# Low parts of weights all on VectorE from the output projection on, and the first feed-forward weights split earlier

## Chip, cores and metric

The kernel runs on one core of a Trainium2 chip. The metric is device time in microseconds (us), the median of several executions; lower is better. Engines: TensorE (PE) multiplies, VectorE (DVE) and ScalarE (ACT) work on vectors, GpSimd (POOL) does too but can't read PSUM, SyncE (SP) only starts DMAs. Each engine takes its instructions in order.

## What is computed

One layer of a hybrid block on x (512 x 1024, float32): token mixing with three branches, cross-attention into 256 memory tokens, a SwiGLU feed-forward, each inside two RMS norms with a residual. Cut to its core:

```python
h = rms_norm(x, g_mix_pre)
lru_x, lru_gate, pool_in, q, k, v, q_idx, k_idx, w_idx, gate_logits = split_columns(h @ w_in, IN_SIZES)
up = einsum(stack([ya, yb, yc]), w_branch)            # ya, yb, yc: the three mixers
merged = sum(sigmoid(gate_logits + b_gate) * up)
x = x + rms_norm(merged @ w_out, g_mix_post)
h = rms_norm(x, g_mem_pre); m = rms_norm(mem, g_mem_kv)
q = h @ w_mem_q; k, v = split(m @ w_mem_kv, 2)        # 4 heads of 128
o = softmax(q @ k.T * 128 ** -0.5) @ v
x = x + rms_norm(o @ w_mem_o, g_mem_post)
h = rms_norm(x, g_ffn_pre)
f_gate, f_up = split(h @ w_ffn_in, 2)                 # 2816 columns each
x = x + rms_norm((silu(f_gate) * f_up) @ w_ffn_out, g_ffn_post)
```

## The kernel before

**Products in three parts.** Each float32 operand is cut into a rounded high part and a low part, the rest. `mm3` (L89 to L92) issues three matmuls for a product: high by high, high by low, low by high. So every weight needs a split ahead of its matmuls. `split_next` (L182) does it: ScalarE casts `raw` to the high part `wh` (L191), then the low part `wl` = raw - wh is made either by one VectorE subtraction over 1024 columns (L195) or by two GpSimd subtractions over 512 each (L198, L199). Which of the two is a list: `low_on("v")` sends all that follow to VectorE, `"g"` all to GpSimd, `"vg"` one after the other.

**Weights in a row.** The weights are a fixed list of 128x1024 pieces: ..., eight of w_out, four K and four V pieces of w_mem_kv, four of w_mem_q, four of w_mem_o, then the feed-forward's. In the names they are numbered: w_out 59 to 66, K 67 to 70, V 71 to 74, w_mem_q 75 to 78, w_mem_o 79 to 82, feed-forward 83 on. Six `raw` buffers are loaded by SyncE as they come free, that is after the low part is made; there are four buffers for high and four for low parts. `take_w` hands out the next weight and splits two ahead; `prefetch(n)` splits up to n ahead. The first four feed-forward weights (`NFIRST`) go into free larger buffers (`K8`), so these can be split before the four pairs are free.

**The stretch around the change.** TensorE's work in program order: the output projection (`project`, hold 2: the last two weights are done row block by row block, t = 0 to 3); K (m = 0 to 3) and V (i = 0 to 3) of the memory; the four heads of w_mem_q with scores, softmax and the products with V (`mem_scores`, `mem_tr`, `mem_av`); w_mem_o (hold 4); the first four feed-forward weights in two column halves (rows 0 to 255 of the tokens, then 256 to 511).
Between them runs a chain per row block, class `Residual`, called R[t]: sums of squares on ScalarE (L286) and the gain on VectorE (L907), the inverse root `rstd` (VectorE L271, L273, L275; GpSimd's power step L274; VectorE L278, L279), the residual (L923), squares again, `rstd` again, the normalised rows (L932), then `turn`: transposes on TensorE (L294), high part `hh` on ScalarE (L302) and low part `hl` on VectorE (L303). The next product reads `hh` and `hl`. `halves` (L392, L393) cuts a PSUM result the same way on ScalarE and VectorE.

**What sets the order.** The program is written in one sequence; a list scheduler puts it into a fixed order per engine at build time, by priority (roughly the place in the program, with splits raised or lowered by `high_priority`) and by its own estimate of times. So a changed engine for one step can move others past each other.

Of the kernel before, what the change touches and what calls it, by code (L numbers as in the profile page):

```python
# [18 lines left out]
KD = D // P  # L19
# [11 lines left out]
NFIRST = 4  # L31
# [34 lines left out]
def hybrid_block_kernel(ctx: ExitStack, tc: tile.TileContext, a: dict, out: bass.AP):  # L66
# [22 lines left out]
    def mm3(o, lh, ll, rh, rl, start, stop):  # L89
        T.matmul(o, lh, rh, start=start, stop=False, skip_group_check=True)  # L90
        T.matmul(o, lh, rl, start=False, stop=False, skip_group_check=True)  # L91
        T.matmul(o, ll, rh, start=False, stop=stop, skip_group_check=True)  # L92
# [6 lines left out]
    def pump(ns):  # L99
        while bg and ns > 0:  # L100
            cost, fn = bg.popleft()
            fn()
            ns -= cost

    def drain_bg():
        while bg:
            bg.popleft()[1]()
# [71 lines left out]
    def low_on(engines):  # L179
        low[:] = engines  # L180

    def split_next(pin=False):  # L182
        src = raws.popleft()
        shape = list(specs[state["split"]][0])
        if first_ffn <= state["split"] < first_ffn + NFIRST:
            both = K8.take([P, 2] + shape[1:], F32R)
            h, l, back = both[:, 0], both[:, 1], lambda: K8.give(both)
        else:
            th, tl = WH.take(shape, F32R), WL.take(shape, F32R)
            h, l, back = th, tl, lambda: (WH.give(th), WL.give(tl))  # L190
        copy = A.copy(h, src)  # L191
        if pin:
            tc.keep_in_program_order(copy)
        if low[state["low"] % len(low)] == "v":
            V.tensor_sub(l, src, f32(h))  # L195
        else:
            c = shape[1] // 2
            G.tensor_sub(l[:, :c], src[:, :c], f32(h[:, :c]))  # L198
            G.tensor_sub(l[:, c:], src[:, c:], f32(h[:, c:]))  # L199
        state["low"] += 1  # L200
        RAW.give(src)
        state["split"] += 1
        ready.append((h, l, back))
        load_ahead()

    def prefetch(ahead=None, pin=False):
        want = state["taken"] + (LOOKAHEAD if ahead is None else ahead)
        while (state["split"] < min(len(specs), want) and raws
               and (WH.free or first_ffn <= state["split"] < first_ffn + NFIRST)):
            with tc.high_priority(offset=-100):  # L210
                split_next(pin)

    def take_w(ahead=None):
        while state["split"] <= state["taken"]:
            split_next()
        w = ready.popleft()
        state["taken"] += 1
        prefetch(ahead)
        return w

    def give_w(*ws):
        for w in ws:
            w[2]()
# [159 lines left out]
    def unit_piece(o, w, c0, c1, ks=range(KD)):  # L383
        for k in ks:
            mm3(o[:, c0:c1], w[0][:, k], w[1][:, k], hh[:, k, c0:c1], hl[:, k, c0:c1], k == 0, k == KD - 1)

    def unit(o, w):
        unit_piece(o, w, 0, S)
        give_w(w)

    def halves(src, h, l):
        A.copy(h, src)  # L392
        V.tensor_sub(l, src, f32(h))  # L393
# [91 lines left out]
    for m in range(1, 4):  # L485
        w = take_w()
        ps = PS.take([P, S])
# [14 lines left out]
    w = take_w()  # L502
    ps = PS.take([P, S])
# [25 lines left out]
    for i, name in enumerate(("lru_w_a", "lru_w_x")):  # L529
        t = T2.take([P, 4, P])  # L530
# [6 lines left out]
    t = T2.take([P, 4, P])  # L537
# [108 lines left out]
    for m in range(4):  # L646
        w = take_w()
        ps = PS.take([P, S])
# [5 lines left out]
    for g in GROUPS:  # L654
        w = take_w()
        ps = PS.take([P, S])
# [9 lines left out]
    for m in range(4):  # L666
        w = take_w()
        ps = PS.take([P, S])
# [140 lines left out]
    for m in range(4):  # L809
        w = take_w()  # L810
        ps = PS.take([P, S])
# [46 lines left out]
        bg.append((1, f))  # L858
    low_on("vg")
    branch(2, yc, lambda: pump(1))  # L860
    low_on("g")
    drain_bg()
    K8.give(*yc, *acc, mem)
    GB.give(g_kv)
# [98 lines left out]
    for m in range(4):  # L963
        w = take_w()
        ps = PS.take([P, NM])
# [19 lines left out]
    for i in range(4):  # L985
        w = take_w()
        for kk in range(2):
            k = 2 * i + kk
# [6 lines left out]
        if i == 2:  # L995
            R[2].turn()
    R[3].turn()
    low_on("v")
    for t in range(2):
        halves(pv[t], vmem[:, 0, t], vmem[:, 1, t])  # L1000
    PS.give(*pv)
# [9 lines left out]
    def mem_scores(h):  # L1011
        mx, sm = col(4, "mx4"), col(4, "sm4")
        pss = []
        for i in range(2):
            ps = PS.take([P, 2, NM])
            pss.append(ps)
            for j in range(2):
                r = slice((2 * i + j) * P, (2 * i + j + 1) * P)
                mm3(ps[:, j], qm[0][:, h, r], qm[1][:, h, r], kmem[:, 0, h], kmem[:, 1, h], True, True)
            V.tensor_reduce(mx[:, 2 * i:2 * i + 2], ps, axis=AX.X, op=OP.max)  # L1020
        V.tensor_scalar(mx, mx, -mscale, None, op0=OP.mult)
        pt = [T2.take([P, 2, NM]) for _ in range(2)]
        for t in range(4):
            A.activation(pt[t // 2][:, t % 2], pss[t // 2][:, t % 2], AF.Exp, bias=mx[:, t:t + 1], scale=mscale,
                         accum_out=sm[:, t:t + 1])
        V.reciprocal(sm, sm)
        for t in range(4):
            p_ = pt[t // 2][:, t % 2]
            V.tensor_scalar(p_, p_, sm[:, t:t + 1], None, op0=OP.mult)
        PS.give(*pss)  # L1030
        mprob[h] = pt

    def mem_tr(h):
        pt = mprob.pop(h)
        hl_ = K8.take([P, 2, 2, S], F32R)
        for kb in range(2):
            ps = PS.take([P, S])
            for t in range(4):
                T.transpose(ps[:, t * P:(t + 1) * P], pt[t // 2][:, t % 2, kb * P:(kb + 1) * P], ident)
            halves(ps, hl_[:, 0, kb], hl_[:, 1, kb])  # L1040
            PS.give(ps)
        T2.give(*pt)
        mprob[h] = hl_
# [11 lines left out]
    for h in range(4):  # L1055
        w = take_w()
        ps = PS.take([P, S])
        for k in range(KD):
            mm3(ps, w[0][:, k], w[1][:, k], hh[:, k], hl[:, k], k == 0, k == KD - 1)
            if k == 5 and h >= 1:  # L1060
                mem_scores(h - 1)
            if k == 5 and h >= 2:
                mem_tr(h - 2)
        give_w(w)
        halves(ps, qm[0][:, h], qm[1][:, h])
        PS.give(ps)
    low_on("vg")
    mem_av(0)
    mem_av(1)
    mem_scores(3)  # L1070
    K8.give(*qm, kmem)
    mem_tr(2)

    HH.give(hh)
    HL.give(hl)
# [2 lines left out]

    def after_o(t, pss):
        R.append(Residual(t, pss, g_post, g_next))  # L1080
        if t == 0:
            low_on("g")
            prefetch(4 + NFIRST)
        if t == 2:
            R[0].scale2()
            R[0].norm()
        if t >= 1:
            R[t - 1].add()
            R[t - 1].square()
        R[t].scale()  # L1090
# [51 lines left out]
        if c == 0:  # L1142
            R[3].turn()
    give_w(*ws)
    low_on("g")
    for m in range(NFIRST // 2):
        swiglu(m, pss[2 * m], pss[2 * m + 1])
    GB.give(g_post, g_next)
    g_post = gain("g_ffn_post")
    for m in range(NFIRST // 2, NFF):  # L1150
        if m == NFIRST // 2 + 1:
            low_on("v")
        w0, w1 = take_w(), take_w()
        pg, pu = PS.take([P, S]), PS.take([P, S])
        unit(pg, w0)
        unit(pu, w1)
        swiglu(m, pg, pu)
# [52 lines left out]
```

## Time and profile before

| | us |
|---|---|
| median of 3 runs | 917.13 (917.04 to 917.58) |
| profiled execution | 914.67 |
| its span, first to last instruction | 912.9 |
| TensorE busy (4179 matmuls) | 885.9, 97% of the span |
| VectorE busy | 499.8, 55% |
| ScalarE busy | 344.3, 38% |
| GpSimd busy | 231.2, 25% |
| subtractions of low parts: VectorE L195, 79 of them | 98.2 |
| GpSimd L198 and L199, 65 pairs | 88.9 and 91.8 |

Busy times are sums over an engine; matmuls overlap a little, and their ends are modelled. Stretches of the trace: the output projection ends at 437.7 us, K and V run to about 467, the heads to about 510, w_mem_o to 537.7, then the feed-forward. A timeline row gives start, duration, engine, line, operation and tiles, and in brackets the engine's idle time before it with what ended it. Buffer numbers are left out of tile names there.

### The profile page before, as it was taken

What the parts mean: (1) busy time and instruction counts of PE and PEld (TensorE: products, weight loads), DVE (VectorE), ACT (ScalarE), POOL (GpSimd) and SP (SyncE); (2) the same over time, 40 slices, a digit from 0 to 9 for tenths busy, and PEclk for the clock granted to TensorE, in tenths of its full rate; (3) what the DMA queues carried; (4) which work ended last, traced back from release to release, by engine and by line L of the source; (5) the groups of instructions that cost most, each with busy time, mean ns of one, the idle gap of its engine ahead of it and who ended that gap; (6) DMA issues with size and microseconds to landing.
All of it is one profiled execution on the core that took longest, in us unless ns stands there. A gap on an engine that the chain in (4) does not pass through costs nothing.

```text
span 912.9 us, 11068 instructions
## 1 busy us (share of the span) xinstructions
PE 885.9 (97%) x4179; PEld 730.5 (80%) x4179; DVE 499.8 (55%) x889; ACT 344.3 (38%) x575; POOL 231.2 (25%) x203
## 2 busy tenths in 40 slices
PE   7999999999999999999989989999999999999997
PEld 6788888888788788888868779888888888888885
DVE  5769989946773745311876783433334443222225
ACT  4465553225654544322655452222223222211121
POOL 2223464644444322344561460000000000000000
PEclk9999999999999999999999999999999999999999
DMA  8953237333332245333454230333333332333102
GB/s 245 242 128 93 70 93 184 93 94 91 104 81 77 75 150 185 96 107 97 117 161 115 70 116 1 93 93 98 104 97 93 93 93 92 96 99 104 48 1 93
DMA packets 122801, 95.42 MB, mean 105 GB/s; under 512 B 5568, under 2 KB 111612, under 8 KB 122748
## 3 DMA queue, kind: packets, MB, share of 16 engines
q1 hardware_dynamic: 120172, 90.52, 34.5%
q10 hardware_dynamic: 2576, 4.19, 1.3%
q8 instruction: 33, 0.54, 0.2%
q14 instruction: 20, 0.16, 0.1%
HBM read 86.83 MB, written 2.10 MB: 97 GB/s over the span
## 4 chain that ended last, share of the span: by engine, by line
PE 88%; DVE 5%; issue 2%; ACT 2%; POOL 1%; DMA 1%; ACTq 0%; DVEq 0%; SPq 0%; POOLq 0%
PE ps L91 28%; PE ps L90 28%; PE ps L92 28%; PE ps L450 1%; PE ps L775 1%; PE ps L760 1%; PE ps L294 1%; DVE wl L195 1%; DVE hl L303 1%; DVE k L932 1%; POOL wl L199 1%; POOL y L274 1%; DVE c L278 0%; DVE k L393 0%; DMA k<-t 0%
## 5 line engine op out<-in xcount | busy, mean ns | idle before, releaser
L191 ACT CAST wh<-raw 128x1024 fp32r<-128x1024 f32 (+1 forms) x144 | 150.5, 1047 | 388.9 <-issue 154.3
L91 PE MATMUL ps<-hl,wh 128*128 128x512 f32 (+2 forms) x736 | 285.5, 388 | 3.7 <-DVE hl L303 3.7
L90 PE MATMUL ps<-hh,wh 128*128 128x512 f32 (+2 forms) x736 | 285.9, 389 | 0.3 <-ACT hh L302 0.3
L92 PE MATMUL ps<-hh,wl 128*128 128x512 f32 (+2 forms) x736 | 285.4, 388 | 0.0
L195 DVE TENSOR_TENSOR wl<-raw,wh 128x1024 fp32r<-128x1024 f32 x79 | 98.2, 1243 | 163.0 <-ACT wh L191 163.0
L91 PEld LDWEIGHTS ps<-hl,wh 128*128 128x128 f32 (+1 forms) x736 | 137.6, 187 | 34.0 <-DVE hl L303 4.6
L90 PEld LDWEIGHTS ps<-hh,wh 128*128 128x128 f32 (+1 forms) x736 | 137.4, 187 | 30.0 <-ACT hh L302 0.5
L92 PEld LDWEIGHTS ps<-hh,wl 128*128 128x128 f32 (+1 forms) x736 | 137.5, 187 | 29.7
L198 POOL TENSOR_TENSOR wl<-raw,wh 128x512 fp32r<-128x512 f32 (+1 forms) x65 | 88.9, 1368 | 199.4 <-ACT wh L191 178.2
L274 POOL TENSOR_TENSOR y<-u,half 128x1 f32<-128x1 f32 x26 | 15.1, 587 | 415.5 <-DVE u L271 384.6
L199 POOL TENSOR_TENSOR wl<-raw,wh 128x512 fp32r<-128x512 f32 (+1 forms) x65 | 91.8, 1412 | 0.0
L90 PE MATMUL ps<-wh,k 128*128 128x512 f32 x192 | 75.8, 395 | 0.0
L91 PE MATMUL ps<-wl,k 128*128 128x512 f32 x192 | 75.5, 393 | 0.0
L92 PE MATMUL ps<-wh,k 128*128 128x512 f32 x176 | 69.7, 396 | 0.0
L90 PE MATMUL ps<-k,wh 128*128 128x512 f32 (+1 forms) x128 | 47.2, 369 | 0.0
L1128 DVE TENSOR_TENSOR t<-t,ps 128x512 f32<-128x512 f32 x22 | 15.1, 688 | 58.5 <-PE ps L92 58.5
L92 PE MATMUL ps<-k,wl 128*128 128x512 f32 (+1 forms) x128 | 46.9, 366 | 0.0
L92 PE MATMUL ps<-wh,x 128*128 128x512 f32 x112 | 44.2, 395 | 0.0
L91 PEld LDWEIGHTS ps<-wl,k 128*128 128x128 f32 x192 | 36.1, 188 | 8.1
L90 PEld LDWEIGHTS ps<-wh,k 128*128 128x128 f32 x192 | 36.0, 188 | 8.2
L92 PEld LDWEIGHTS ps<-wh,k 128*128 128x128 f32 x176 | 33.4, 190 | 8.1 <-DVE k L393 0.2
L90 PE MATMUL ps<-wh,x 128*128 128x512 f32 x96 | 38.8, 404 | 0.0
(210 smaller groups left out, 1173.7 us busy)
## 6 DMA issues: line engine op xcount, KB each, us to landing
raw<-in_w_in SPq DMA_DIRECT2D x45, 512.0 KB, 4.0
raw<-in_w_ffn_in SPq DMA_DIRECT2D x44, 512.0 KB, 3.8
raw<-in_w_ffn_out SPq DMA_DIRECT2D x22, 512.0 KB, 3.5
raw<-in_w_branch SPq DMA_DIRECT2D x12, 512.0 KB, 3.4
k<-t SPq DMA_DIRECT2D x32, 128.0 KB, 2.4
raw<-in_w_out SPq DMA_DIRECT2D x8, 512.0 KB, 3.6
raw<-in_w_mem_kv SPq DMA_DIRECT2D x8, 512.0 KB, 3.6
k<-in_x ACTq DMA_DIRECT2D x2, 1024.0 KB, 8.9
```

What stands on the lines that cost most here:

```text
L90: T.matmul(o, lh, rh, start=start, stop=False, skip_group_check=True)
L91: T.matmul(o, lh, rl, start=False, stop=False, skip_group_check=True)
L92: T.matmul(o, ll, rh, start=False, stop=stop, skip_group_check=True)
L191: copy = A.copy(h, src)
L195: V.tensor_sub(l, src, f32(h))
L198: G.tensor_sub(l[:, :c], src[:, :c], f32(h[:, :c]))
L199: G.tensor_sub(l[:, c:], src[:, c:], f32(h[:, c:]))
L274: G.tensor_tensor(y, u, half, op=OP.pow)
L294: T.transpose(ps[:, k], src[:, (4 * q + k) * P:(4 * q + k + 1) * P], ident)
L303: V.tensor_sub(hl[:, 4 * q:4 * q + 4, dst], ps, f32(h))
L450: T.matmul(ps[:, :n], q[j][:, hp, r], k[i][:, :n], start=i == 0, stop=i == 1, skip_group_check=True)
L1128: V.tensor_mul(th, th, pu)
```

## The change

`low_on("v")` now stands right behind the third branch, where `low_on("g")` stood, and the later switches are gone: every low part from weight 61 on is made by VectorE (the first ones of these while the third branch still runs). 24 weights move: 61 to 76, 82, 84 to 86 and 87 to 90. The first head of w_mem_q is multiplied in two column halves of 256 tokens, 48 matmuls instead of 24. `prefetch(4 + NFIRST)` is called ahead of w_mem_o instead of behind its first row block. (With h = 0 the scores call of the loop isn't reached, so `h >= 1` is no longer written.)

```diff
--- before.py
+++ after.py
@@ -858,7 +858,7 @@
         bg.append((1, f))
     low_on("vg")
     branch(2, yc, lambda: pump(1))
-    low_on("g")
+    low_on("v")
     drain_bg()
     K8.give(*yc, *acc, mem)
     GB.give(g_kv)
@@ -995,7 +995,6 @@
         if i == 2:
             R[2].turn()
     R[3].turn()
-    low_on("v")
     for t in range(2):
         halves(pv[t], vmem[:, 0, t], vmem[:, 1, t])
     PS.give(*pv)
@@ -1055,21 +1054,24 @@
     for h in range(4):
         w = take_w()
         ps = PS.take([P, S])
-        for k in range(KD):
+        if h == 0:
+            for c in range(2):
+                unit_piece(ps, w, c * 256, c * 256 + 256)
+        for k in range(KD) if h else ():
             mm3(ps, w[0][:, k], w[1][:, k], hh[:, k], hl[:, k], k == 0, k == KD - 1)
-            if k == 5 and h >= 1:
+            if k == 5:
                 mem_scores(h - 1)
             if k == 5 and h >= 2:
                 mem_tr(h - 2)
         give_w(w)
         halves(ps, qm[0][:, h], qm[1][:, h])
         PS.give(ps)
-    low_on("vg")
     mem_av(0)
     mem_av(1)
     mem_scores(3)
     K8.give(*qm, kmem)
     mem_tr(2)
+    prefetch(4 + NFIRST)
 
     HH.give(hh)
     HL.give(hl)
@@ -1078,9 +1080,6 @@
 
     def after_o(t, pss):
         R.append(Residual(t, pss, g_post, g_next))
-        if t == 0:
-            low_on("g")
-            prefetch(4 + NFIRST)
         if t == 2:
             R[0].scale2()
             R[0].norm()
@@ -1142,14 +1141,11 @@
         if c == 0:
             R[3].turn()
     give_w(*ws)
-    low_on("g")
     for m in range(NFIRST // 2):
         swiglu(m, pss[2 * m], pss[2 * m + 1])
     GB.give(g_post, g_next)
     g_post = gain("g_ffn_post")
     for m in range(NFIRST // 2, NFF):
-        if m == NFIRST // 2 + 1:
-            low_on("v")
         w0, w1 = take_w(), take_w()
         pg, pu = PS.take([P, S]), PS.take([P, S])
         unit(pg, w0)
```

VectorE between the K and V parts of the memory. First the order before: behind the low part of row block 0 (`hl_2`) come the inverse roots and normalised rows (`k_4`, `k_5`) of blocks 2 and 3, and K's low parts.

```order
L273 TENSOR_SCALAR u<-ss 128x1 x2
L275 TENSOR_SCALAR w<-u 128x1 x2
L278 SCALAR_TENSOR_TENSOR c<-y,w 128x1 x2
L279 SCALAR_TENSOR_TENSOR y<-c,y 128x1 x2
L932 SCALAR_TENSOR_TENSOR k_4_44_3880<-k_2_41_3596,y,gb_4_3601 128x1024
L393 TENSOR_TENSOR k_6_46_3954<-ps_197_4058,k_6_46_3954 128x256
L932 SCALAR_TENSOR_TENSOR k_5_45_3911<-k_2_41_3596,y,gb_4_3601 128x1024
L393 TENSOR_TENSOR k_6_46_3954<-ps_198_4102,k_6_46_3954 128x256
L303 TENSOR_TENSOR hl_2_3604<-ps_201_4150,hh_2_3603 128x4x128
```

The same place with the change:

```order
L273 TENSOR_SCALAR u<-ss 128x1
L393 TENSOR_TENSOR k_6_46_3944<-ps_197_4047,k_6_46_3944 128x256
L275 TENSOR_SCALAR w<-u 128x1
L273 TENSOR_SCALAR u<-ss 128x1
L195 TENSOR_TENSOR wl_71_4042<-raw_71_3737,wh_71_4041 128x1024
L278 SCALAR_TENSOR_TENSOR c<-y,w 128x1
L275 TENSOR_SCALAR w<-u 128x1
L195 TENSOR_TENSOR wl_72_4085<-raw_72_3767,wh_72_4084 128x1024
L279 SCALAR_TENSOR_TENSOR y<-c,y 128x1
L278 SCALAR_TENSOR_TENSOR c<-y,w 128x1
L932 SCALAR_TENSOR_TENSOR k_4_44_3872<-k_2_41_3596,y,gb_4_3601 128x1024
L279 SCALAR_TENSOR_TENSOR y<-c,y 128x1
```

The subtractions of the first two V weights (71, 72) stand between the inverse roots and the normalised rows; before, GpSimd made them.

VectorE ahead of the feed-forward, before: the inverse roots, the normalised rows of block 1 (`k_6_61`) right behind them, then the low part of block 0 (`ps_239`, `ps_240`).

```order
L275 TENSOR_SCALAR w<-u 128x1
L278 SCALAR_TENSOR_TENSOR c<-y,w 128x1 x2
L279 SCALAR_TENSOR_TENSOR y<-c,y 128x1 x2
L932 SCALAR_TENSOR_TENSOR k_6_61_4713<-k_7_40_3595,y,gb_6_4255 128x1024
L303 TENSOR_TENSOR hl_3_4577<-ps_239_4795,hh_3_4576 128x4x128
L303 TENSOR_TENSOR hl_3_4577<-ps_240_4800,hh_3_4576 128x4x128
```

With the change:

```order
L303 TENSOR_TENSOR hl_3_4617<-ps_240_4804,hh_3_4616 128x4x128
L273 TENSOR_SCALAR u<-ss 128x1
L195 TENSOR_TENSOR wl_83_4897<-raw_87_4588,wh_83_4896 128x1024
L275 TENSOR_SCALAR w<-u 128x1
L195 TENSOR_TENSOR wl_84_4903<-raw_88_4594,wh_84_4902 128x1024
L278 SCALAR_TENSOR_TENSOR c<-y,w 128x1
L907 TENSOR_TENSOR x_1_63_4855<-ps_237_4791,gb_5_4237 128x512
L279 SCALAR_TENSOR_TENSOR y<-c,y 128x1
L907 TENSOR_TENSOR x_1_63_4855<-ps_238_4792,gb_5_4237 128x512
L932 SCALAR_TENSOR_TENSOR k_6_61_4717<-k_7_40_3595,y,gb_6_4239 128x1024
L278 SCALAR_TENSOR_TENSOR c<-y,w 128x1
L271 TENSOR_SCALAR u<-ss 128x1
```

The low part of block 0 (the row of `ps_240` is the last of it), two subtractions (weights 87, 88, by the number of `raw`) and block 3's gain (`ps_237`, `ps_238`) now stand ahead of the normalised rows of block 1, and another subtraction (89) behind them.

TensorE at the same place, before: the transposes of block 1 (`ps_241`, `ps_242`), then the last weight of w_mem_o (82) for block 3.

```order
L90 MATMUL ps_238_4788<-wh_81_4578,x_2_50_4259 128x512
L91 MATMUL ps_238_4788<-wl_81_4579,x_2_50_4259 128x512
L92 MATMUL ps_238_4788<-wh_81_4578,k_0_51_4260 128x512
L294 MATMUL ps_241_4831<-ident,k_6_61_4713 128x128 x4
L294 MATMUL ps_242_4836<-ident,k_6_61_4713 128x128 x4
L90 MATMUL ps_237_4787<-wh_82_4584,x_2_50_4259 128x512
L91 MATMUL ps_237_4787<-wl_82_4585,x_2_50_4259 128x512
L92 MATMUL ps_237_4787<-wh_82_4584,k_0_51_4260 128x512
L90 MATMUL ps_238_4788<-wh_82_4584,x_2_50_4259 128x512
```

With the change:

```order
L90 MATMUL ps_237_4791<-wh_82_4590,x_2_50_4243 128x512
L91 MATMUL ps_237_4791<-wl_82_4591,x_2_50_4243 128x512
L92 MATMUL ps_237_4791<-wh_82_4590,k_0_51_4244 128x512
L90 MATMUL ps_238_4792<-wh_82_4590,x_2_50_4243 128x512
L91 MATMUL ps_238_4792<-wl_82_4591,x_2_50_4243 128x512
L92 MATMUL ps_238_4792<-wh_82_4590,k_0_51_4244 128x512
L294 MATMUL ps_241_4835<-ident,k_6_61_4717 128x128 x4
L294 MATMUL ps_242_4840<-ident,k_6_61_4717 128x128 x4
L90 MATMUL ps_243_4908<-hh_3_4616,k_3_55_4596 128x256
```

The matmuls with weight 82 now stand ahead of the transposes, and the first matmuls of the feed-forward (`hh_3`) right behind them.

## Rows read from the trace of the kernel before

**Rows 1.** Windows; busy us of each engine (instructions), granted clock, DMA share, GB/s
```profile
436.00:475.00 39.00, 32.96 (x202) 28.19 (x202) 34.06 (x51) 21.37 (x36) 27.11 (x22) 1.00 0.47 150
475.00:510.00 35.00, 34.33 (x184) 28.64 (x183) 23.95 (x46) 21.85 (x53) 10.07 (x8) 1.00 0.42 116
510.00:551.00 41.00, 38.19 (x224) 32.85 (x224) 32.70 (x61) 18.63 (x38) 16.23 (x16) 0.96 0.27 80
```

**Rows 2.** Waits of TensorE, 395 to 580 us: total, times, longest
```profile
PE ps L294 <- DVE k L932: 3.9, 3, 2.8
PE ps L91 <- DVE hl L303: 2.9, 1, 2.9
```

**Rows 3.** Timeline of TensorE: start, duration, instruction, idle before and its releaser
```profile
437.68 0.28 PE L90 MATMUL ps<-k,wh 128*128 128x256 f32 x1
...
445.31 1.06 PE L294 MATMUL ps<-ident,k 128*128 128x128 f32 x8 [1.80 <-DVE y L279]
...
471.18 0.50 PE L91 MATMUL ps<-hl,wh 128*128 128x512 f32 x1 [2.85 <-DVE hl L303]
...
480.50 0.28 PE L90 MATMUL ps<-k,x 128*128 128x256 f32 x1
```

**Rows 4.** Timeline of VectorE, 429 to 455 us
```profile
429.48 1.39 DVE L907 TENSOR_TENSOR k<-ps,gb 128x512 f32<-128x512 f32 x2 [33.11 <-ACT k L286]
...
435.37 0.22 DVE L278 SCALAR_TENSOR_TENSOR c<-y,w 128x1 f32<-128x1 f32 x1 [0.48 <-POOL y L274]
...
437.02 1.28 DVE L907 TENSOR_TENSOR k<-ps,gb 128x512 f32<-128x512 f32 x2
...
438.22 0.21 DVE L271 TENSOR_SCALAR u<-ss 128x1 f32<-128x1 f32 x1
...
440.23 1.25 DVE L278 SCALAR_TENSOR_TENSOR c<-y,w 128x1 f32<-128x1 f32 x1 [1.55 <-POOL y L274]
...
443.89 1.27 DVE L932 SCALAR_TENSOR_TENSOR k<-k,y,gb 128x1024 f32<-128x1024 f32 x1
...
446.53 0.41 DVE L393 TENSOR_TENSOR k<-ps,k 128x256 fp32r<-128x256 f32 x1
```

**Rows 5.** Timeline of GpSimd (POOL), 434 to 447 us
```profile
434.79 0.55 POOL L274 TENSOR_TENSOR y<-u,half 128x1 f32<-128x1 f32 x1 [3.17 <-DVE u L271]
...
440.17 1.29 POOL L199 TENSOR_TENSOR wl<-raw,wh 128x512 fp32r<-128x512 f32 x1
...
445.43 1.52 POOL L274 TENSOR_TENSOR y<-u,half 128x1 f32<-128x1 f32 x1 [1.49 <-DVE u L271]
```

**Rows 6.** Timelines: a subtraction on VectorE, and TensorE's last transposes of heads
```profile
476.84 1.23 DVE L195 TENSOR_TENSOR k<-raw,k 128x1024 fp32r<-128x1024 f32 x1 [3.99 <-ACT k L191]
...
509.92 1.23 PE L1039 MATMUL ps<-ident,t 128*128 128x128 f32 x8 [0.67 <-DVE t L1029]
```

**Rows 7.** Timelines of TensorE, then VectorE, before the feed-forward
```profile
527.30 1.03 PE L294 MATMUL ps<-ident,k 128*128 128x128 f32 x8
...
533.94 1.38 PE L294 MATMUL ps<-ident,k 128*128 128x128 f32 x8 [2.81 <-DVE k L932]
534.97 0.78 PE L90 MATMUL ps<-wh,x 128*128 128x512 f32 x1
...
537.67 0.41 PE L90 MATMUL ps<-hh,k 128*128 128x256 f32 x1
...
523.70 1.28 DVE L932 SCALAR_TENSOR_TENSOR k<-k,y,gb 128x1024 f32<-128x1024 f32 x1
...
528.86 1.40 DVE L278 SCALAR_TENSOR_TENSOR c<-y,w 128x1 f32<-128x1 f32 x2 [0.61 <-POOL y L274]
...
531.42 2.37 DVE L932 SCALAR_TENSOR_TENSOR k<-k,y,gb 128x1024 f32<-128x1024 f32 x1
```

**Rows 8.** Windows, TensorE alone: busy us, granted clock, DMA share, GB/s
```profile
470.00:471.00 1.00, 0.00 (x0) 1.00 0.27 107
535.00:536.00 1.00, 1.00 (x5) 0.50 0.00 2
```

## Prediction

> **What bounds the kernel now.** I read the stretches first [rows 1], then TensorE's waits [rows 2], then the timelines at those waits. TensorE is the bound: outside 436 to 551 us it hardly pauses between the start and the last store, so only that stretch can pay. In its three parts TensorE is busy 32.96 of 39, 34.33 of 35 and 38.19 of 41 us, about 9.5 us idle [rows 1]. The waits say for whom: VectorE's normalised rows (L932, and at 445.31 the small L279 ahead of one) before the transposes, and its low part of the features (L303) [rows 2, 3].
>
> The reader should see why VectorE is late. Up to 437 us its tiny 128x1 step L278 takes 0.22 us; at 440.23 the same step takes 1.25, and it ends with a GpSimd half subtraction that ran from 440.17 for 1.29 [rows 4, 5]. The same shows at 528.86 (two take 1.40) and at 531.42 (2.37 for a step that takes 1.27 elsewhere) [rows 4, 7]. So while GpSimd subtracts, VectorE stands, though its queue is not full.
>
> **The sum's base.** The profiled execution took 914.67 us (span 912.9 and 1.8 around it), 2.5 less than the median of 917.13; I take differences from its trace and put them on the median.
>
> **Part 1: 24 low parts go from GpSimd to VectorE.** Each took two GpSimd instructions of about 1.29 [rows 5] and becomes one VectorE instruction of 1.23 [rows 6]; I count 1.15 from start to start. The first eight (the last six of w_out, the first two of w_mem_kv) fall between 388 and 429 us, where VectorE has next to nothing to do: its L907 at 429.48 ends a wait of 33.11 [rows 4]. They cost nothing: a weight is ready 1.3 us earlier than with two GpSimd halves. If that cover were gone, each would cost up to 1.15.
>
> From 437 on VectorE is full, so I walk its new queue against TensorE's. Prices, start to start: 1.2 for a 128x1024 step or a pair of 128x512 (437.02 to 438.22), 0.35 for L393, 0.12 to 0.25 for a small step, 1.15 for a subtraction [rows 4, 6]. TensorE: 0.233 for a 512-column matmul (40 from 471.18 to 480.50), 0.12 for 256 columns (48 from 437.68 to 443.5, where the idle of 1.80 begins) [rows 3], 0.8 for eight transposes.
>
> (a) From 437.02: pair 1.2, two small 0.25, the subtraction of the third K weight 1.15, pair 1.2, some six small 0.9, then L932 of row block 0. It starts at 441.8 where it started at 443.89, and ends at 443.0 to 443.4. TensorE gets there at 443.5: the idle of 1.80 goes.
> (b) Then L923, L393, subtraction of the fourth K weight, L923, L393, L932 of block 1 and about seven small: 6.2 us, end 449.2 to 450.2. TensorE finishes the K half at 450.0, so the transposes of block 1 don't wait.
> (c) Then the L303 pair, L393, four small, and only then the subtraction of the first V weight, which ended on GpSimd before it was wanted: 1.2 + 0.35 + 0.4 + 1.15 puts it at 452.2 to 453.4. TensorE, after two matmuls of the high part and six transposes, wants it at 451.0. That is a **new wait of 1.2 to 2.4 us**; behind it in TensorE's queue stand the whole V half and w_mem_q.
> (d) Then a subtraction, L932, L393, L932, the L303 pair and the third V weight's subtraction: 7 us, 459.1 to 460.9; TensorE is there at 459.0 to 460.2: 0.1 to 0.7 more.
> (e) Three subtractions, two L303 pairs and two L393 end at 467.4 to 469.3. With the first head of w_mem_q in two column halves, TensorE needs row blocks 0 and 1 for the first half (464.9 to 466.8) and blocks 2 and 3 only 2.9 us later, at 467.8 to 469.7. The wait of 2.85 at 471.18 goes; the halves cost 48 x 0.12 against 24 x 0.233, 0.1 us.
> The first score matmul, now at 480.50 [rows 3], comes at 474.8 to 476.7: **3.8 to 5.7 us gained, I take 4.7**, the middle, since nothing in the trace says which side. The ends differ by GpSimd's power step (L274), which stays on GpSimd: 0.55 alone, 1.52 where it started inside a VectorE step of 1.27 at 445.43 [rows 5]. The late end gives it such a delay three times (0.4 to 0.5 each, what L278 would then wait).
>
> The Trainium skill bears on this ("SBUF — State Buffer", section "Who interferes with whom"): a VectorE instruction with two SBUF inputs and a GpSimd instruction that reads SBUF exclude one another, and whichever starts first holds for its whole length. Row 440.23 agrees, and so does the power step. By that rule the moved subtractions, which have two SBUF inputs, now hold up the power step, which speaks for the late end, 3.8; without it the early end, 5.7, would stand.
>
> **Part 2: heads and prefetch.** The part from 475 to 510 has VectorE busy 23.95 of 35 [rows 1]; four more subtractions (4.6 us) fit. Those of the second pair of feed-forward weights stand ahead of the last head's normalisation, which ends some 0.6 us later; but the scheduler puts eleven matmuls (2.6 us) of the output projection ahead of the transposes that waited 0.67 at 509.92 [rows 6]. I take **0.7 gained**, between 0.3 and 0.9. Moving the prefetch call itself costs nothing: the loads follow freed buffers on SP's queue, and these come free about as much earlier as TensorE is; the loads of w_mem_o and of the first feed-forward weights (raw buffers freed by the subtractions of (c) to (e)) move up by some 4 us with it.
>
> **Part 3: start of the feed-forward.** Here four subtractions come into the queue in a bad place. Before, TensorE waited from 531.13 to 533.94 for L932 of block 1, then ran eight transposes and six matmuls at half speed (0.43 each) and began the feed-forward at 537.67 [rows 7]. Now L932 of block 0 ends at 527.5 (it started at 523.70 [rows 7]; its sums finish 2.1 us later, since nine matmuls of block 1 come first, and part of block 1's L907 pair, 0.5, goes ahead of it; 526.3 + 1.2), just when TensorE wants it at 527.3. Behind it: L907 pair, L923, L303 pair, two subtractions, L907 pair, L932 of block 1 and some eight small, 1.2 x 5 + 1.15 x 2 + 0.9 = 9.2: it ends at 536.6 to 537.0, against 533.8 now. The six matmuls now go before these transposes, so TensorE runs dry at 532.5 and waits **4.1 to 4.5 us**. Another subtraction stands ahead of L303 of block 1, so the first low-part matmul starts at 538.8 to 539.2, where the same point, four matmuls on from 537.67, lies at 538.35 now: 0.5 to 0.9 lost.
> To that comes the clock. Behind the idle of 2.81 it was at 0.50 in 535 to 536; behind the idle of 2.85 in 468 to 471 it stayed at 1.00 [rows 8]. Six matmuls in 2.70 instead of 1.40 [rows 7] are 1.3 us lost, 1.5 with the transposes, already inside the 537.67. A longer idle may cost the same again behind it or be over by then: 0 to 1.9, I take 1.0. Together **1.7 lost**, between 0.5 and 2.8.
> From there on nothing differs but buffers; blocks 2 and 3 are normalised 1 to 2 us before they are wanted.
>
> **Sum.** 4.7 + 0.7 - 1.7 = 3.7 us gained: 917.13 - 3.7 = 913.4 (911.0 for a profiled execution like this one). With the ends, gains of 1.3 (3.8 + 0.3 - 2.8) to 6.1 (5.7 + 0.9 - 0.5).
>
> **Rivals.** *Better:* every part at its good end, 6.1: 911.0. For it: what stretched VectorE's steps by a microsecond each is gone. Against it: VectorE has no slack left, so small delays add up.
> *No change:* the new wait for the first V weight is the longer one and brings half clock with it, as at 534: 3.8 - 1.5 + 0.3 - 2.8 = -0.2, so 917.3. For it: of the two idle spells of 2.8 us one was followed by half clock.
> *Slower, by the power step:* each L278 stands behind a power step that itself stood behind a subtraction, at 0.97 (1.52 - 0.55) a time. There are some nine of them on the two chains; from four on the gain is gone, at six it is 3.7 - 5.8, 919.2. Against it: in my walk other steps lie between most pairs.
> *The change doesn't do what it says:* VectorE's small steps stay long without GpSimd's subtractions. Then 34.06 us of VectorE work in 436 to 475 [rows 1] plus eight subtractions of 1.15 is 43.3 in 39, 4.2 later: 921.3. The coincidence at 440.17 speaks against it.
>
> **How the numbers follow.** About 0.2% (1.8 us) is what a measurement of this kernel can tell from no change. Forecast, 912 to 915.3: 0.48. Better: 0.19. No change: 0.23. Slower: power step 0.08, the last rival 0.02. So faster 0.67, same 0.23, slower 0.10. The range leaves out the slower cases and the outer tail of the better: 909.8 to 917.6.
>
> **What would show it.** Right: L278 back at 0.2 to 0.4 from 437 on; L932 of block 0 no longer waited for; a new TensorE wait of 1 to 3 us on L195 about 13 us after the K half starts; no wait on L303 at the first head; an idle of 4 us or more before block 1's transposes at the feed-forward, with half clock about it. Wrong: VectorE idle between 440 and 468 (then the chain is elsewhere), TensorE waits on L195 above 4 us, or power steps above 1 us in number.

## The result

The changed kernel takes **909.67 us** where the kernel before took 917.09: a ratio of 0.9917, 95% interval 0.9898 to 0.9937. The 909.67 is the median of four executions (908.77, 909.26, 910.08 and a slow one of 2573.08, which the ratio leaves out; the other three have a median of 909.26). A second measurement, the run e10 below, gave 908.91 against 917.03, again 0.9917 (0.9904 to 0.9931). So it is faster, as forecast, but by 7.4 us where 3.7 were forecast, and just outside the range of 909.8 to 917.6 on its fast side. The profiled execution took 908.77 (span 906.7), 5.9 less than the one of before (914.67).

Windows of the changed kernel, for the same three parts as [rows 1], cut earlier because each part now comes earlier (us, busy us of PE, PEld, DVE, ACT and POOL with instructions, granted clock, DMA share, GB/s):

```profile
436.00:470.00 34.00, 33.56 (x233) 30.68 (x232) 31.27 (x59) 21.53 (x37) 5.05 (x6) 1.00 0.58 179
470.00:505.00 35.00, 35.00 (x191) 29.93 (x190) 28.13 (x53) 21.29 (x53) 0.00 (x0) 1.00 0.41 115
505.00:545.00 40.00, 36.37 (x209) 31.49 (x208) 28.97 (x61) 18.55 (x38) 7.28 (x8) 0.91 0.27 78
```

The first two stretches have lost nearly all of TensorE's idle time. GpSimd's 27 us of the memory stretch have become 5. The idle that is left, 3.6 us, lies in the third, and that one has the lower mean clock. Its waits, 395 to 580 us, against [rows 2]:

```profile
PE ps L294 <- DVE c L278: 3.5, 1, 3.5
PE ps L91 <- DVE wl L195: 0.4, 1, 0.4
PE ps L90 <- ACT hh L302: 0.2, 1, 0.2
```

The waits of 1.80 and 2.85 [rows 3] are gone. The new one on L195, for which the prediction asked 1.2 to 2.4 us, is 0.44. The timeline of TensorE at the places of [rows 3] and [rows 7] (start, duration, instruction, idle before it and its releaser):

```profile
437.38 0.28 PE L90 MATMUL ps<-k,wh 128*128 128x256 f32 x1
...
451.31 0.50 PE L91 MATMUL ps<-wl,k 128*128 128x512 f32 x1 [0.44 <-DVE wl L195]
...
473.87 0.28 PE L90 MATMUL ps<-k,x 128*128 128x256 f32 x1
...
520.71 0.48 PE L90 MATMUL ps<-wh,x 128*128 128x512 f32 x1
...
528.65 1.94 PE L294 MATMUL ps<-ident,k 128*128 128x128 f32 x8 [3.50 <-DVE c L278]
...
557.52 0.40 PE L91 MATMUL ps<-hl,wh 128*128 128x512 f32 x1
```

These are the K half's start, the first V weight, the first score, the matmuls behind block 0's transposes ahead of the feed-forward, block 1's transposes, and the first matmul of 512 columns of the fifth and sixth feed-forward weights. VectorE, against [rows 4]:

```profile
440.75 0.35 DVE L278 SCALAR_TENSOR_TENSOR c<-y,w 128x1 f32<-128x1 f32 x2
...
441.21 1.28 DVE L932 SCALAR_TENSOR_TENSOR k<-k,y,gb 128x1024 f32<-128x1024 f32 x1
...
447.15 1.27 DVE L932 SCALAR_TENSOR_TENSOR k<-k,y,gb 128x1024 f32<-128x1024 f32 x1
...
450.05 1.21 DVE L195 TENSOR_TENSOR wl<-raw,wh 128x1024 fp32r<-128x1024 f32 x1
...
456.70 2.34 DVE L195 TENSOR_TENSOR wl<-raw,wh 128x1024 fp32r<-128x1024 f32 x2
...
464.60 1.29 DVE L303 TENSOR_TENSOR hl<-ps,hh 128x512 fp32r<-128x512 f32 x2 [0.35 <-ACT hh L302]
```

Two L278 together take 0.35 where one took 1.25 [rows 4]. Every row of the walk is earlier than the prediction put it: L932 of block 0 starts at 441.21 (forecast 441.8), that of block 1 ends at 448.42 (449.2 to 450.2), the first V weight's subtraction at 451.26 (452.2 to 453.4), the third's, the first of the pair at 456.70, at about 457.9 (459.1 to 460.9), and the last L303 at 465.89 (467.4 to 469.3).

### The profile page after: what moved, and what is told of

Its sections match the earlier page's. It is cut to its first block, busy times and chain, and to the rows that moved or that the text cites. A ratio compares the mean times of both kernels' runs of the same rounds, so it can differ in the third digit from the quotient of the medians.

```text
span 906.7 us, 11059 instructions
## 1 busy us (share of the span) xinstructions
PE 885.4 (98%) x4203; PEld 732.9 (81%) x4203; DVE 507.0 (56%) x913; ACT 344.4 (38%) x575; POOL 169.2 (19%) x155
## 4 chain that ended last, share of the span: by engine, by line
PE 88%; DVE 7%; issue 2%; ACT 1%; DMA 1%; POOL 1%; ACTq 0%; DVEq 0%; POOLq 0%
PE ps L90 28%; PE ps L91 28%; PE ps L92 28%; PE ps L450 2%; DVE k L907 1%; PE ps L775 1%; PE ps L294 1%; DVE k L923 1%; DVE hl L303 1%; DVE wl L195 1%; PE ps L760 1%; DVE k L932 1%; ACT k L286 0%; PE ps L1038 0%; POOL y L274 0%
## 5 line engine op out<-in xcount | busy, mean ns | idle before, releaser
L191 ACT CAST wh<-raw 128x1024 fp32r<-128x1024 f32 (+1 forms) x144 | 150.5, 1048 | 393.0 <-issue 169.2
L195 DVE TENSOR_TENSOR wl<-raw,wh 128x1024 fp32r<-128x1024 f32 x100 | 122.8, 1230 | 191.2 <-ACT wh L191 191.2
L274 POOL TENSOR_TENSOR y<-u,half 128x1 f32<-128x1 f32 x26 | 18.9, 731 | 526.8 <-DVE u L271 478.5
L198 POOL TENSOR_TENSOR wl<-raw,wh 128x512 fp32r<-128x512 f32 (+1 forms) x44 | 59.6, 1355 | 153.1 <-ACT wh L191 138.9
L91 PE MATMUL ps<-wl,k 128*128 128x512 f32 x160 | 63.0, 394 | 0.4 <-DVE wl L195 0.4
L199 POOL TENSOR_TENSOR wl<-raw,wh 128x512 fp32r<-128x512 f32 (+1 forms) x44 | 61.4, 1396 | 0.0
L90 PE MATMUL ps<-wh,x 128*128 128x512 f32 x128 | 50.7, 396 | 0.0
L91 PE MATMUL ps<-wl,x 128*128 128x512 f32 x128 | 50.3, 393 | 0.0
L92 PEld LDWEIGHTS ps<-wh,k 128*128 128x128 f32 x208 | 39.1, 188 | 9.2 <-DVE k L393 0.2
L91 PE MATMUL ps<-k,wh 128*128 128x512 f32 x96 | 37.9, 395 | 0.0
L91 PEld LDWEIGHTS ps<-wl,k 128*128 128x128 f32 x160 | 30.0, 188 | 7.5 <-DVE wl L195 0.7
```

The source lines that it names most:

```text
L274: G.tensor_tensor(y, u, half, op=OP.pow)
```

## The experiments

**e1: the kernel before, unchanged.** The forecast's base was a profiled execution of 914.67 us, when others of the same kernel took 917. Where is the difference?

> The kernel before, unchanged, to learn where its usual executions differ from the profiled one (914.67 us, mean granted clock 0.997; the others 916.1 to 917.6). Theory: they hold about 2 us more of half clock, behind the idle of 2.85 that ends at 471.18, so their mean clock is 0.994 to 0.996, and a profile of such an execution shows 0.50 somewhere in 471 to 476 with the first score matmul 1 to 2 us later than 480.50. Rival: the clock is 0.997 in all of them and the 2 us lie elsewhere (start, transfers, a stretch outside 436 to 551).

Eleven runs gave 916.43 us (914.31 to 918.18), 0.9996 of the kernel before (0.9987 to 1.0005). The profiled one took 916.17. Its TensorE, at the idle of [rows 3] and at four marks from the K half to the feed-forward, and then its windows behind that idle (us, busy us of PE, granted clock, DMA share, GB/s):

```profile
437.71 0.28 PE L90 MATMUL ps<-k,wh 128*128 128x256 f32 x1
...
471.19 0.79 PE L91 MATMUL ps<-hl,wh 128*128 128x512 f32 x1 [2.86 <-DVE hl L303]
...
481.98 0.28 PE L90 MATMUL ps<-k,x 128*128 128x256 f32 x1
...
529.57 0.48 PE L90 MATMUL ps<-wh,x 128*128 128x512 f32 x1
...
564.78 0.40 PE L91 MATMUL ps<-hl,wh 128*128 128x512 f32 x1
```

```profile
471.00:472.00 1.00, 0.81 (x2) 0.50 0.53 82
...
474.00:475.00 1.00, 1.00 (x5) 0.81 1.16 336
```

The idle is the same to 0.01 us and ends at the same time, but TensorE comes out of it at 0.50, the lower of its two levels (1.2 GHz), and the 40 matmuls up to the first score take 10.79 us where [rows 3] have 9.32. These 1.47 us are the whole difference between this execution (916.17) and the one the forecast rested on (914.67). So the theory holds for this execution. Of the 26 executions of this kernel timed on that chip only one, 914.31, was as short as the forecast's base, and only that one has its mean clock, 0.997; the others have 0.990 to 0.995. On the chip of e5 the short kind was more frequent: four of 17 took 914.5 to 915.3, at 0.993 to 0.996. Not all of that is this place: in the first 20 us the clock of this execution is lower too, which costs nothing at the K half (437.71 against 437.68). That the others hold half clock behind the idle as well fits their times, but none of them was profiled, and what separates them further, up to 918.18, is not located.

**e2: the changed kernel without the column halves.**

```
-        if h == 0:
-            for c in range(2):
-                unit_piece(ps, w, c * 256, c * 256 + 256)
-        for k in range(KD) if h else ():
+        for k in range(KD):
```

> The changed kernel with the first head of the memory query in one piece of 512 columns again. Theory (the halves cover the last row block): TensorE stands at the first head from about 464.0 to the end of L303 of block 3 at 465.9, a wait on L303 of 1.8 to 2.0 us, so 1.7 to 1.9 us slower than the changed kernel (909.7): 911.4 to 911.6, up to 913 if half clock follows the idle. Rival (the low parts on VectorE alone do it, and the halves give nothing because a later wait takes the time back): 909.7, no new wait above 0.5 us.

909.47 us, 0.9919 of before (0.9907 to 0.9931): no slower. TensorE, K half, first head and first score:

```profile
438.12 0.28 PE L90 MATMUL ps<-k,wh 128*128 128x256 f32 x1
...
465.35 0.73 PE L90 MATMUL ps<-hh,wh 128*128 128x512 f32 x2 [0.40 <-ACT hh L302]
...
475.43 0.28 PE L90 MATMUL ps<-k,x 128*128 128x256 f32 x1
```

The expected wait of 1.9 us is one of 0.40, on ScalarE: by the time TensorE asks for VectorE's low part, that is there. From the K half to the first score it takes 37.31 us instead of 36.49, so the halves give 0.8 in the trace. The medians don't show it; in this execution about as much comes back later, since from block 0's transposes to the fifth feed-forward weight, the last two marks of the changed kernel's timeline, it takes 35.78 instead of 36.81. So the low parts on VectorE make the gain, with the earlier prefetch call beside them; no run takes that call back alone.

**e11: the same question in a steadier kernel** (e8 below, without the halves).

> The version with the feed-forward's later low parts behind all four normalisations, and the first head of the memory query in one piece again: what the column halves are worth once the low parts are moved, without the half clock at the feed-forward that blurred this in the changed kernel. Theory (the trace of the first such comparison holds: 0.40 of waiting on ScalarE's L302, and transposes that take 1.32 instead of 0.7): 0.7 to 0.9 us slower than with the halves, 906.2 to 906.5 against 905.5. Rival (worth nothing): 905.3 to 905.8.

905.37 us (903.57 to 907.38) against e8's 905.54. Again 0.80 in the stretch: the transposes of block 0 start at 441.30 and the first score at 472.93, 31.63 us, where e8 has 443.55 and 474.38, 30.83.

But this execution had arrived there 2.25 us earlier: in the first 45 us TensorE waited 2.8 us for L316 in it, and 5.9 in e8's. Such differences in the start hide 0.8 us in a median. Neither expectation is settled by the time; by the trace the halves are worth 0.8.

**e5: the halves alone, on the kernel before** (the first edit of the change's heads, and nothing else).

```
-        for k in range(KD):
+        if h == 0:
+            for c in range(2):
+                unit_piece(ps, w, c * 256, c * 256 + 256)
+        for k in range(KD) if h else ():
```

> The kernel before with one edit of the change alone: the first head of the memory query in two column halves. Theory (in the kernel before, the halves fill the idle of 2.85 before L303 of block 3, and take away the 3 us of half clock that nearly all its executions hold behind it): 2.3 to 2.7 us of wait and 1.5 of clock, 912.7 to 913.3 against 917.0; the gains of halves and low parts overlap, since with the low parts moved the halves gave nothing. Rival (the halves are worth as little here as there): 916 to 917, the wait on L303 only moves to the second half.

915.57 us, 0.9985 (0.9971 to 0.9998), in two groups: six executions of 913.6 to 914.8 and six of 916.3 to 917.7. The profiled one, 917.53, is of the second. TensorE, then ScalarE, then the queue that issues loads:

```profile
470.81 0.39 PE L91 MATMUL ps<-hl,wh 128*128 128x256 f32 x1 [0.90 <-DVE hl L303]
...
480.22 0.39 PE L90 MATMUL ps<-k,x 128*128 128x256 f32 x1 [2.29 <-ACT x L392]
...
477.69 1.05 ACT L191 CAST k<-raw 128x1024 fp32r<-128x1024 f32 x1 [9.06 <-DMA raw<-in_w_ffn_in]
479.59 0.58 ACT L392 CAST x<-ps 128x512 fp32r<-128x512 f32 x1
...
470.62 2.27 SPq L173 DMA_DIRECT2D raw<-in_w_ffn_in x2
```

The wait of 2.86 shrinks to 0.90, and the 2 us come back as 2.29 at the first score. The copy of the first head's queries (L392) stands on ScalarE behind the copy of a feed-forward weight (L191), which stands 9.06 us for its load; that load was issued only at 470.62, right behind one that had waited for GpSimd's subtraction (L199, until 470.17) to free a raw buffer. With the low parts moved, the same queue issues its feed-forward loads from 463.68 on, and the same L191 starts at 469.56. So the moved subtractions also bring the loads forward; alone, the halves gain a third of what was expected. The late issue is not all of this wait, though: the kernel before issued that load at 470.94, still later, and copied it at 475.75, 4.81 us after (5.05 in e1), where here it took 7.07. Why the load was slower in this execution is not shown. Whether the shorter half of the executions is free of this wait was not profiled.

**e6: one weight's low part back on GpSimd.** The third K weight, which VectorE subtracts at 438.11.

```
-        if low[state["low"] % len(low)] == "v":
+        if low[state["low"] % len(low)] == "v" and state["split"] != 68:
```

> The changed kernel with one low part, that of the third K weight of w_mem_kv (VectorE 438.11, 1.22 us), back on GpSimd as two halves. Theory (while GpSimd subtracts, VectorE's small steps wait for it): VectorE is rid of 1.15 us, but L278 and L279 between 439 and 443 take 1.2 to 2.4 us instead of 0.15 to 0.35, L932 of block 0 starts at 441.5 to 443.5, no earlier than the 441.21 of the changed kernel; 909.5 to 911.0. Rival (only the number of steps in VectorE's queue counts): the small steps stay at 0.15 to 0.35, L932 of block 0 starts at about 440.1, and all that follows on VectorE is 1.1 earlier; 908.7 to 909.7, since TensorE hardly waits there.

910.41 us (909.68 to 913.34), 0.9939 (0.9925 to 0.9954). GpSimd, VectorE, TensorE:

```profile
439.73 1.31 POOL L199 TENSOR_TENSOR wl<-raw,wh 128x512 fp32r<-128x512 f32 x1
...
439.80 1.25 DVE L278 SCALAR_TENSOR_TENSOR c<-y,w 128x1 f32<-128x1 f32 x1 [1.55 <-POOL y L274]
...
442.37 1.28 DVE L932 SCALAR_TENSOR_TENSOR k<-k,y,gb 128x1024 f32<-128x1024 f32 x1
...
452.81 0.50 PE L91 MATMUL ps<-wl,k 128*128 128x512 f32 x1 [1.83 <-DVE wl L195]
...
476.00 0.28 PE L90 MATMUL ps<-k,x 128*128 128x256 f32 x1
```

The row of 1.25 under [rows 4] is back: L278 ends with GpSimd's second half. VectorE first waits 1.55 for the power step, which is queued between the two halves on GpSimd. Rid of 1.15 us of work, VectorE reaches L932 of block 0 1.16 us later than with it, the wait for the first V weight grows from 0.44 to 1.83, and the K half to the first score takes 38.75 us (437.25 to 476.00) instead of 36.49. That is 2.3 us for one weight. The median shows 0.7 to 1.5 of it (against 909.67 and 908.91). In the profiled execution the feed-forward's start gives 1.0 back: it takes 35.84 us between the same two marks instead of 36.81, with half clock from about 530.6 to 534.1, shorter than in the changed kernel.

**e3: the feed-forward's low parts back on GpSimd.**

```
+    low_on("g")
     ws = [take_w() for _ in range(NFIRST)]
@@
     for m in range(NFIRST // 2, NFF):
+        if m == NFIRST // 2 + 1:
+            low_on("v")
```

> The changed kernel with the low parts that are made at the start of the feed-forward (those of its fifth to eighth weight matrix and two more) on GpSimd again, as in the kernel before. Theory (the subtractions ahead of L932 of block 1 cost more on VectorE than as halves on GpSimd): the wait before block 1's transposes goes from 3.50 to about 2.8 us and the half clock behind it from 6 to some 3.5 us, 1.7 to 2 us faster than the changed kernel: 907.7 to 908.0. Rival (GpSimd's halves hold VectorE's small steps as long as the moved subtractions do): wait 3.3 to 3.7 us, 909.7.

911.75 us, 0.9943 (0.9931 to 0.9956): slower by 2.1 than the changed kernel (2.8 against e10), where 1.7 to 2 faster was expected; the rival's "as long" falls short too. VectorE, then TensorE:

```profile
525.33 2.43 DVE L278 SCALAR_TENSOR_TENSOR c<-y,w 128x1 f32<-128x1 f32 x2 [1.85 <-POOL y L274]
527.68 2.52 DVE L279 SCALAR_TENSOR_TENSOR y<-c,y 128x1 f32<-128x1 f32 x2
...
531.54 1.94 PE L294 MATMUL ps<-ident,k 128*128 128x128 f32 x8 [6.68 <-DVE k L932]
```

Four small steps that take 0.6 together elsewhere take 4.95, one GpSimd half each, and L932, at 530.12, ends at 531.4 instead of 528.5. The kernel before got off with a wait of 2.81 [rows 7]: there GpSimd's first half started only at 528.95, and stretched one step of each pair (1.40 for two L278 [rows 7], 1.31 for two L279) and L932.

**e4: the same low parts on VectorE, but later.** They belong to the fifth to eighth feed-forward weight, wanted from 557 on. Here they are held, in program order, behind block 2's norm and block 3's sum.

```
-        if pin:
-            tc.keep_in_program_order(copy)
@@
-            V.tensor_sub(l, src, f32(h))
+            sub = V.tensor_sub(l, src, f32(h))
+            if pin:
+                tc.keep_in_program_order(sub)
@@
     R[3].scale2()
     K8.give(*om)
+    prefetch(4 + NFIRST, pin=True)
@@
-    ws = [take_w() for _ in range(NFIRST)]
+    ws = [take_w(0) for _ in range(NFIRST)]
```

> The changed kernel with those low parts of the feed-forward's fifth to eighth weight matrix left on VectorE but put behind L932 and L923 of block 2, since they are wanted only some 30 us later. Theory (they were all that made L932 of block 1 late): L932 of block 1 ends at about 525.5 instead of 528.5, the wait before its transposes is 0.3 to 1.2 us instead of 3.50, the 6 us of half clock behind it go or shrink to 2: 2.5 to 6 us faster than the changed kernel, 904 to 907. Rival (block 1's sums of squares on ScalarE are late anyway): a wait of 2 to 3 us stays, now on ScalarE or GpSimd's power step, and the time is 908.5 to 909.7.

906.17 us, 0.9882 (0.9868 to 0.9895). TensorE, and its windows about the first wait:

```profile
527.01 1.06 PE L294 MATMUL ps<-ident,k 128*128 128x128 f32 x8 [0.99 <-DVE k L932]
...
542.38 1.09 PE L294 MATMUL ps<-ident,x 128*128 128x128 f32 x8 [1.06 <-DVE x L932]
```

```profile
526.00:528.00 2.00, 1.01 (x9) 1.00 0.03 8
528.00:530.00 2.00, 1.50 (x10) 1.00 0.00 0
```

The wait of 3.50 becomes 0.99, and the clock stays at 1.00 behind it. The three subtractions that now stand ahead of block 3's L932 cost 1.06 there. The edit has a side effect: one earlier call, in the kernel's first part, also pins, and there too the subtraction is now held instead of ScalarE's copy. The gain doesn't come from that: the K half starts later than in the changed kernel (438.30 against 437.38).

**e8: the same, later still**, behind the low part of block 3. The prefetch of e4 goes into the feed-forward's first loop:

```
         if c == 0:
             R[3].turn()
+            prefetch(4 + NFIRST, pin=True)
```

> The version with the feed-forward's later low parts on VectorE, these now behind L303 of block 3, and so behind all four normalisations. Theory: the wait of 1.06 us before block 3's transposes goes, that of 0.99 before block 1's stays, nothing else changes: 905.0 to 905.4 against 906.2. Rival (now the fifth weight is late): its subtraction ends after TensorE wants it at about 555, a wait on the subtraction of over 1 us, 906 to 908.

905.54 us (905.15 to 906.85), 0.9882 (0.9869 to 0.9895). Its waits, 395 to 580 us, then TensorE at the last two marks of the changed kernel's timeline:

```profile
PE ps L294 <- DVE k L932: 1.0, 1, 1.0
...
PE ps L91 <- DVE wl L193: 0.5, 1, 0.5
```

```profile
521.23 0.48 PE L90 MATMUL ps<-wh,x 128*128 128x512 f32 x1
...
553.97 0.40 PE L91 MATMUL ps<-hl,wh 128*128 128x512 f32 x1
```

The wait for block 3 is gone; the one on the subtraction (here L193) is that for the first V weight, and none for the fifth feed-forward weight has come, as the theory said. Between the two marks it takes 32.74 us, where e4 takes 34.01 and the changed kernel 36.81; the medians of e4 and e8 lie only 0.6 apart. This version beats both kernels.

**e9: e8 with block 1's residual added ahead of block 2's products.**

```
-        R.append(Residual(t, pss, g_post, g_next))
         if t == 2:
             R[0].scale2()
             R[0].norm()
+            R[1].add()
+            R[1].square()
+        R.append(Residual(t, pss, g_post, g_next, t == 3))
-        if t >= 1:
+        if t in (1, 3):
@@
```

The last argument of `Residual` (passed down in lines not shown) holds block 3's products (L907) in program order, so that they don't slip ahead of block 1's rows.

> The same, and at the start of the feed-forward VectorE adds block 1's residual before it multiplies block 2's products (L923 before the L907 pair), with block 3's products held behind block 1's normalisation. Theory: L932 of block 1 starts 1.2 us earlier, the wait of 0.99 and the two of 0.25 behind it go: 903.7 to 904.3. Rival (block 2 is then late by as much): the wait passes to block 2's transposes or to the matmuls of block 3 that want its banks, 905.

908.22 us, 0.9909 (0.9896 to 0.9922): worse than e8. VectorE, TensorE:

```profile
523.54 1.29 DVE L907 TENSOR_TENSOR k<-ps,gb 128x512 f32<-128x512 f32 x2 [1.80 <-ACT k L286]
...
528.81 1.64 PE L294 MATMUL ps<-ident,k 128*128 128x128 f32 x8 [2.88 <-DVE k L934]
```

The sum of block 1 does come earlier (520.46, in e4 521.75), but behind it VectorE waits 1.80 for ScalarE (L286), and block 1's rows (here L934) start at 527.39, 1.8 later than in e4, not 1.2 earlier. Both expectations missed this wait.

**e10: the changed kernel again.**

> The changed kernel again, for a closer time beside the kernel before on one chip. Theory (the gain against the forecast is real, and consists of a stretch 1.9 us better than priced and 1.5 of half clock that the forecast's base did not hold): 909.2 to 910.3, a ratio of 0.991 to 0.993; the waits of 0.44 and 3.50 again, the half clock behind the latter between 3 and 6 us long. Rival (the first measurement was lucky): 911 to 913.4.

908.91 us (908.52 to 910.95), a little below the expected band, with the same ratio as before. Its waits are those of the changed kernel, with 3.51 for 3.50. So the first measurement was not lucky.

## Why the prediction was half of it

Two things failed: the base that the differences were taken from, and the sizes of the terms (c) and (d) of part 1. They hid 1.5 and 1.6 us of gain. The mechanism held.

The marks of e1 and of the changed kernel, executions of 916.17 and 908.77, locate 7.3 of their 7.4 us: 0.33 up to the K half (437.71 to 437.38; the same program up to there starts it at 437.03 in e10 and 438.12 in e2, so this lies within the scatter of the start), 7.78 from there to the first score (44.27 us to 36.49), 0.75 in the heads (47.59 to 46.84), and 1.60 lost at the feed-forward's start (35.21 to 36.81).

**The base was wrong by 1.5.** The prediction saw that one idle of 2.8 us was followed by half clock and another was not [rows 8], and took the second for a property of the place. It was not: e1 has half clock behind the same idle. Taking differences from the one trace and putting them on the median left out a gain that the change makes in executions like e1's, and by their times and mean clocks most are like it; only e1's was profiled. The 2.5 us by which the profiled execution was below the median were the hint, and they were set aside.

**Part 1 was under-sized: 4.7 forecast, 6.3 measured** on the forecast's own base (42.82 us of [rows 3] to 36.49), outside its 3.8 to 5.7. The order of the walk held row by row, and (a) and (e) came true: the waits of 1.80 and 2.85 went. What failed are the prices. Small steps were put at 0.12 to 0.25 each, and the seven between 440.50 and 441.21 took 0.10 each; the power-step delays of the late end came to nothing. With a start 0.3 earlier the rows of the walk lie 0.6 us ahead of the forecast at its beginning and 1.5 to 3.4 at its end. So term (c) was 0.44, not 1.2 to 2.4, and term (d) nothing, not 0.1 to 0.7. Taken from the middle of their ranges they miss by 1.36 and 0.4, which is 1.8, about the missing 1.6. In (e) the halves were taken to be needed; e2 and e11 show that, the low parts moved, they give 0.8, and e5 that alone they gain 1.4.

**The power step did not come through.** It was to be held by the moved subtractions and to hold L278 in turn, which was the late end of part 1 and the slower rival. GpSimd in the changed kernel, then VectorE's waits in 436 to 475 of before, and in 436 to 470 of after:

```profile
438.21 2.04 POOL L274 TENSOR_TENSOR y<-u,half 128x1 f32<-128x1 f32 x2 [3.17 <-DVE u L273]
...
449.75 1.91 POOL L274 TENSOR_TENSOR y<-u,half 128x1 f32<-128x1 f32 x2 [5.04 <-DVE u L273]
```

```profile
DVE c L278 <- POOL y L274: 2.8, 4, 1.6
```

```profile
DVE hl L303 <- ACT hh L302: 0.4, 1, 0.4
```

The first half is right: two power steps take 2.04 and 1.91, where one alone takes 0.55 [rows 5]. So far the trace agrees with what the prediction took from the Trainium skill ("SBUF — State Buffer", "Who interferes with whom"): while a VectorE instruction reads two operands from SBUF, a GpSimd instruction that reads SBUF stands. The second half is wrong: VectorE waited 2.8 us for the power step before and not at all now, because other steps stand between in its order. What holds the critical engine was removed, what holds the idle one costs nothing.

**The mechanism was right.** That GpSimd's halves stretch VectorE's small steps was inferred from coincidences; e6 and e3 show it by putting halves back: 1.25 for one L278, 4.95 for four small steps, and 2.3 us of the stretch for one weight. "While GpSimd subtracts, VectorE stands" was too wide, though. The steps that are stretched (L278, L279, L923, L932) read two tiles from SBUF. Beside GpSimd's half of 437.88 to 439.17, VectorE's L271 with one input took 0.21 at 438.22 [rows 4], and beside the half from 441.42 the pair of L907, with one input in PSUM, took 1.27 at 441.40. "The change doesn't do what it says" is refuted by L278 at 0.35 for two.

**Part 2 was right:** 0.7 forecast, 0.75 measured, and the wait of 0.67 [rows 6] is gone. What the earlier prefetch call has of it was not taken apart.

**Part 3 was right in its sum, 1.7 against 1.6** (35.21 to 36.81 us), **not in its parts.** The wait is 3.50 (4.1 to 4.5 forecast), because the small steps are cheap here too, and the later wait on L303 of block 1 did not come; the clock takes more than the 1.0 allowed. That these misses cancel is luck. TensorE alone, windows behind that idle:

```profile
527.00:528.00 1.00, 0.00 (x0) 0.64 1.09 328
528.00:529.00 1.00, 0.35 (x2) 0.50 1.01 263
...
533.00:534.00 1.00, 1.00 (x7) 0.50 0.56 165
534.00:535.00 1.00, 1.00 (x10) 0.95 0.18 42
```

Half clock lasts from about 527.3 to 534.1 here, 5.4 us of it with TensorE at work, which by the lower level's half speed is an estimated 2.7 lost; behind the idle of 2.81 before it lasted 3.4, all at work, by the same estimate 1.7. The reason given, a bad place in VectorE's queue, was right: e3 put the subtractions back on GpSimd and lost 2.1 more, so it was not the engine. Moved behind the normalisations (e8) they cost nothing visible, the wait shrinks to 1.0 and the half clock is gone: 4.1 us below the changed kernel by the medians, and the same between the two marks.

**The rivals.** "Better", 911.0, was the nearest; it lacked the 1.5 of the base. "No change" needed half clock behind the wait for the first V weight; at 0.44 us that wait brought none.

## What to carry to other kernels

Where one profiled execution is faster than the median by as much as the effect one looks for, find out what the median execution has that this one lacks before taking differences from it; here it was half clock behind an idle that the change removes. When GpSimd and VectorE share a stretch, price GpSimd's work by what it adds to those of VectorE's small dependent steps that read two tiles from SBUF, up to one GpSimd instruction each, not by VectorE's busy time. And a subtraction wanted 30 us later should be held behind the rows that TensorE waits for now: its place was worth 4 us, its engine 2.

## What the runs showed of the hardware

Behind the same idle of 2.85 us, at the same point of the same program, the granted clock was 1.00 in one execution and 0.50 for over three us in another. About a wait of 3.50 it was at 0.50 for over six us in the changed kernel; behind 0.99 and 1.06 (e4) it stayed at 1.00. A GpSimd subtraction of 128x512 held a VectorE step of 128x1 with two inputs in SBUF for its whole 1.3 us (1.25 for L278 in e6), and a chain of four such steps met four of them (4.95 in e3); a step with one input took 0.21 beside such a subtraction. The first 45 us differ by over 2 us between e8 and e11, whose programs differ only later, which is more than some edits here are worth.
